# Three of eight pairs of k-tiles of the SwiGLU products as seven block products in place of eight, with casts of 2048 columns

## Chip, core and metric

The kernel runs on one core of one Trainium2 chip. The metric is device time in microseconds (us). The kernel before takes 1956.91 us, the median of three runs.

## What is computed

One layer of a streaming encoder over 256 rows of width 2048 in f32. Nearly all arithmetic is in the two SwiGLUs (inner width 5632) that open and close the layer, SwiGLU 1 and SwiGLU 2; between them lie a mixing layer (latent attention and gated linear attention) and a cross-attention to 256 memory rows.

```python
def swiglu(h, w_gate, w_up, w_down):
    return (jax.nn.silu(h @ w_gate) * (h @ w_up)) @ w_down
...
        x = x + 0.5 * swiglu(rmsnorm(x, ffn1_norm[l]), ffn1_w_gate[l], ffn1_w_up[l], ffn1_w_down[l])
...
        x = x + jnp.concatenate([o_mla, o_gla], axis=-1) @ w_out[l]
        x = x + memory_cross_attention(rmsnorm(x, mem_attn_norm[l]), rmsnorm(mem, mem_norm[l]),
...
        x = x + 0.5 * swiglu(rmsnorm(x, ffn2_norm[l]), ffn2_w_gate[l], ffn2_w_up[l], ffn2_w_down[l])
```

## The kernel before

Every large product runs in `gemm` (L114). TensorE multiplies in f32r, a rounded f32, so both factors are split into a high and a low part of that type, and three products are summed in PSUM: high by high, high by low, low by high. A k-tile is 128 rows of a weight matrix. For 256 rows of x (two blocks `b` of 128, the stationary tiles) and 1024 columns of weights (two halves `c` of 512), one k-tile costs 12 matmuls into the four PSUM banks named `acc`:

```python
L123            o, w = chunks[c]
L124            self.last_pe = nc.tensor.matmul(
```

`slab` (L92) loads two k-tiles, 1 MB, by SyncE's queue into one of three buffers `raw`, and splits each of the two:

```python
L109            self.last_act = nc.scalar.copy(out=wh, in_=src)
L110            self.last_dve = nc.vector.tensor_tensor(out=wl, in0=src, in1=wh.bitcast(F32), op=ALU.subtract)
```

ScalarE casts 1024 columns to the high part `wh`, and VectorE subtracts it from `raw` to give the low part `wl`. There are four buffers of each.

`ffn` (L369) runs a SwiGLU in two groups of inner columns, of six and five *chunks* of 512, numbered 0 to 10. A chunk multiplies all 16 k-tiles of x (its high and low parts are `hth` and `htl`) by 512 columns of gate and 512 of up: 192 matmuls. Then ScalarE evicts the gate with a Silu (L386) and VectorE multiplies by up (L388). Splitting these activations is side work, done during the next chunk: TensorE transposes them (L177), ScalarE casts (L182) and VectorE subtracts (L183), into `acth` and `actl`. After the chunks of a group *down* multiplies the group's 24 or 20 k-tiles of activations by w_down, 1024 columns of output at a time (two such gemms), and VectorE adds the result to the residual `xs` (L404). The rope tables and gains of the mixing layer are set up during chunk 2 of SwiGLU 1 (`setup_mix`): small loads issued by GpSimd, a transpose of the gains (L255), and some 30 small operations on VectorE (L328 among them).

The order on each engine's queue is fixed when the program is built: a scheduler places the instructions by its own estimate of when their inputs are there, and each engine then runs its queue in order. Buffers come from rotating pools, and a tile waits until the readers of its buffer's last content are done.

Of the kernel before, what the change touches and what calls it, by code (L numbers as in the profile page):

```python
# [50 lines left out]

class Kernel:
    def __init__(self, ctx, tc, io):
# [36 lines left out]
    def slab(self, segs, k0, nk, per):  # L90
# [13 lines left out]
        for j in range(0, nk, per):  # L104
            m = min(per, nk - j)
            wh = self.wspl.tile([P, 2 * CW], F32R, name="wh")[:, :m * width]
            wl = self.wspl.tile([P, 2 * CW], F32R, name="wl")[:, :m * width]
            src = flat[:, j * width:(j + m) * width]
            self.last_act = nc.scalar.copy(out=wh, in_=src)  # L109
            self.last_dve = nc.vector.tensor_tensor(out=wl, in0=src, in1=wh.bitcast(F32), op=ALU.subtract)  # L110
# [3 lines left out]
    def gemm(self, x, segs, chunks, ks, ahead=None, side=()):  # L114
# [15 lines left out]
        while i < n:  # L130
            if ahead:
                ahead(i)
            nk = 1 if ahead and i < 2 else min(2 * per, n - i)
            with ExitStack() as first:
                if ahead and not i:
                    for ins in self.first:
                        first.enter_context(self.tc.issue_after(ins))
                parts = self.slab(segs, ks[i], nk, per)
# [21 lines left out]
        return out  # L160

# [32 lines left out]

    def sum_sq(self, src, out, width):
# [3 lines left out]
    def new_ht(self):  # L199
        return [  # L200
            tuple(self.keep.tile([P, 4, S], F32R, name=f"ht{p}{n}") for p in "hl") for n in range(NCH)
        ]

    def norm_chunk(self, src, ht, ss, n, b, g, sq=True):

        self.split_t(src, ht[n], 0, b, 4, g + 4 * n)
        if sq:
            self.sum_sq(src, ss[:, b, n:n + 1], CW)
# [789 lines left out]
```

## Time and profile before

| | |
|---|---|
| median of three runs (lowest to highest) | 1956.91 us (1956.27 to 1957.24) |
| the profiled execution, whole | 1957.86 us |
| its span from first to last instruction | 1956.2 us |
| mean granted TensorE clock, share of full | 0.999 |
| instructions | 22341 |
| weights and other data moved | 356.05 MB, mean 182 GB/s |

The profile is of one execution: times in it are held against its own 1957.86 us, not against the median. Its views give, per engine, busy time and counts; for each group of instructions the time of one and the idle time before it with what ended it; and the chain of work that ended last, followed back from the last instruction.

### The profile page before, as it was taken

What the parts mean: (1) busy time and instruction counts of PE and PEld (TensorE: products, weight loads), DVE (VectorE), ACT (ScalarE), POOL (GpSimd) and SP (SyncE); (2) the same over time, 40 slices, a digit from 0 to 9 for tenths busy, and PEclk for the clock granted to TensorE, in tenths of its full rate; (3) what the DMA queues carried; (4) which work ended last, traced back from release to release, by engine and by line L of the source; (5) the groups of instructions that cost most, each with busy time, mean ns of one, the idle gap of its engine ahead of it and who ended that gap; (6) DMA issues with size and microseconds to landing.
All of it is one profiled execution on the core that took longest, in us unless ns stands there. A gap on an engine that the chain in (4) does not pass through costs nothing.

```text
span 1956.2 us, 22341 instructions
## 1 busy us (share of the span) xinstructions
PE 1940.9 (99%) x8712; PEld 1584.2 (81%) x8712; DVE 1015.8 (52%) x1272; ACT 906.8 (46%) x1277; POOL 58.5 (3%) x114
## 2 busy tenths in 40 slices
PE   8999999999999999999999999999999999999999
PEld 6888888888888888788778878888888888888887
DVE  5555544444545455555565656554444445454443
ACT  6444443334444445665556665544444334444432
POOL 2000000000000000120100020000000000000000
PEclk9999999999999999999999999999999999999999
DMA  7555655555555545554336544555555555565563
GB/s 263 188 186 186 193 194 177 189 194 186 190 186 191 193 173 176 178 159 153 129 128 208 177 153 155 193 180 188 192 193 184 183 192 194 186 192 183 193 208 115
DMA packets 148075, 356.05 MB, mean 182 GB/s; under 512 B 11018, under 2 KB 11120, under 8 KB 147968
## 3 DMA queue, kind: packets, MB, share of 16 engines
q1 hardware_dynamic: 147360, 354.07, 54.8%
q8 instruction: 68, 1.11, 0.2%
q0 software_dynamic: 608, 0.55, 0.1%
q14 instruction: 39, 0.32, 0.0%
HBM read 352.48 MB, written 2.10 MB: 181 GB/s over the span
## 4 chain that ended last, share of the span: by engine, by line
PE 98%; DMA 1%; ACT 1%; POOL 0%; DVE 0%; issue 0%; SPq 0%; ACTq 0%
PE acc L124 93%; PE bank L177 2%; PE bank L743 0%; PE bank L598 0%; PE bank L579 0%; PE bank L742 0%; DMA raw<-in_ffn_w_up_dram 0%; PE bank L797 0%; ACT junk L197 0%; PE bank L806 0%; DMA m<-in_mem_dram 0%; ACT wh L109 0%; PE bank L673 0%; PE bank L808 0%; PE bank L883 0%
## 5 line engine op out<-in xcount | busy, mean ns | idle before, releaser
L110 DVE TENSOR_TENSOR wl<-raw,wh 128x1024 fp32r<-128x1024 f32 (+2 forms) x668 | 809.5, 1216 | 789.0 <-ACT wh L109 787.8
L109 ACT CAST wh<-raw 128x1024 fp32r<-128x1024 f32 (+2 forms) x668 | 695.0, 1046 | 906.6 <-PE acc L124 865.7
L124 PE MATMUL acc<-wh,hth 128*128 128x512 f32 (+1 forms) x1696 | 667.5, 394 | 2.5 <-ACT wh L109 2.5
L124 PE MATMUL acc<-wl,hth 128*128 128x512 f32 (+1 forms) x1696 | 659.1, 389 | 0.0
L124 PE MATMUL acc<-wh,htl 128*128 128x512 f32 (+1 forms) x1696 | 540.6, 388 | 0.0
L124 PEld LDWEIGHTS acc<-wh,hth 128*128 128x128 f32 x1696 | 319.3, 188 | 72.6 <-issue 3.7
L124 PEld LDWEIGHTS acc<-wh,htl 128*128 128x128 f32 x1696 | 318.3, 188 | 65.2
L124 PEld LDWEIGHTS acc<-wl,hth 128*128 128x128 f32 x1696 | 319.4, 188 | 63.0
L124 PE MATMUL acc<-wh,acth 128*128 128x512 f32 x704 | 280.2, 398 | 0.0
L124 PE MATMUL acc<-wl,acth 128*128 128x512 f32 x704 | 279.0, 396 | 0.0
L124 PE MATMUL acc<-wh,actl 128*128 128x512 f32 x704 | 227.1, 396 | 0.0
L124 PEld LDWEIGHTS acc<-wh,actl 128*128 128x128 f32 x704 | 132.7, 188 | 32.3
L124 PEld LDWEIGHTS acc<-wh,acth 128*128 128x128 f32 x704 | 132.6, 188 | 31.9
L124 PEld LDWEIGHTS acc<-wl,acth 128*128 128x128 f32 x704 | 132.6, 188 | 31.7
L388 DVE SCALAR_TENSOR_TENSOR t<-acc,sm,t 128x512 f32<-128x512 f32 x44 | 33.0, 750 | 51.8 <-PE acc L124 46.4
L188 ACT ACTIVATE hth<-bank,gains 128x128 fp32r<-128x128 f32 x128 | 42.3, 366 | 25.8 <-DVE htl L191 19.8
L386 ACT ACTIVATE t<-acc,sm 128x512 f32<-128x512 f32 x44 | 30.4, 691 | 49.7 <-PE acc L124 49.7
L191 DVE SCALAR_TENSOR_TENSOR htl<-bank,gains,hth 128x128 fp32r<-128x128 f32 x128 | 40.2, 345 | 13.2 <-ACT hth L188 13.0
L404 DVE SCALAR_TENSOR_TENSOR xs<-acc,xs 128x512 f32<-128x512 f32 x32 | 21.5, 688 | 17.1 <-PE acc L124 17.1
L183 DVE TENSOR_TENSOR actl<-bank,acth 128x512 fp32r<-128x512 f32 x44 | 30.1, 683 | 0.0
L177 PEld LDWEIGHTS bank<-ident,t 128*128 128x128 f32 x188 | 23.4, 140 | 6.3
L177 PE MATMUL bank<-ident,t 128*128 128x128 f32 x188 | 28.3, 272 | 0.0
(231 smaller groups left out, 989.8 us busy)
## 6 DMA issues: line engine op xcount, KB each, us to landing
raw<-in_ffn_w_down_dram SPq DMA_DIRECT2D x88, 1024.0 KB, 5.1
raw<-in_ffn_w_gate_dram SPq DMA_DIRECT2D x175, 512.0 KB, 3.8
raw<-in_ffn_w_up_dram SPq DMA_DIRECT2D x175, 512.0 KB, 4.7
raw<-in_w_in_dram SPq DMA_DIRECT2D x24, 1024.0 KB, 5.1
raw<-in_w_out_dram SPq DMA_DIRECT2D x16, 1024.0 KB, 5.2
raw<-in_w_in_dram SPq DMA_DIRECT2D x8, 832.0 KB, 4.6
raw<-in_mem_w_k_dram SPq DMA_DIRECT2D x4, 1024.0 KB, 5.1
raw<-in_mem_w_q_dram SPq DMA_DIRECT2D x4, 1024.0 KB, 5.1
```

Of the source, the lines that this page charges most:

```text
L109: self.last_act = nc.scalar.copy(out=wh, in_=src)
L110: self.last_dve = nc.vector.tensor_tensor(out=wl, in0=src, in1=wh.bitcast(F32), op=ALU.subtract)
L124: self.last_pe = nc.tensor.matmul(out=out[b][c][:, :w], lhsT=high, rhs=part[:, o:o + w], start=start, stop=stop)
L177: nc.tensor.transpose(out=t[:, j * P:(j + 1) * P], in_=src[:, j * P:(j + 1) * P], identity=self.ident)
L183: nc.vector.tensor_tensor(out=tl[:, j0:j0 + nj, bs], in0=tv, in1=hv.bitcast(F32), op=ALU.subtract)
L188: h = nc.scalar.activation(out=hv, in_=tv, func=AF.Copy, scale=gv)
L191: nc.vector.scalar_tensor_tensor(out=tl[:, j0 + j, bs], in0=tv, scalar=gv, in1=hv.bitcast(F32), op0=ALU.mult, op1=ALU.subtract)
L386: nc.scalar.activation(out=sg, in_=out[b][0], func=AF.Silu, scale=r)
L388: nc.vector.scalar_tensor_tensor(out=a, in0=out[b][1], scalar=r, in1=sg, op0=ALU.mult, op1=ALU.mult)
L404: nc.vector.scalar_tensor_tensor(out=xc, in0=out[b][c], scalar=0.5, in1=xc, op0=ALU.mult, op1=ALU.add)
```

## The change

Two neighbouring k-tiles form a *pair*. A pair of weight tiles, with two k-tiles as rows and two halves of 512 as columns, and a pair of tiles of x, with two blocks of rows and two k-tiles as columns, are 2 x 2 block matrices. The kernel before multiplies them as eight block products, which with three products of parts each are 24 matmuls. The change takes three of a chunk's eight pairs (1, 3 and 5; in the last group's down two of six: 1 and 3) in seven block products, p1 to p7 (Strassen's scheme in Winograd's form), 21 matmuls. These pairs are called *mixed*, the others *plain*.

- A mixed pair needs sums of weight blocks: VectorE makes four of them, in f32, in one buffer `wsum` (L204 two at once, L209, L210, each from the one before). ScalarE casts 1536 columns of the raw blocks and 2048 columns of the sums, and VectorE makes their low parts (L125). The low part of the sums is called *sum-low* below.
- It needs sums of blocks of x and of the activations too. `split_pair` (L338) makes them from transposed blocks in a buffer `f` on VectorE (L370 to L373) and casts and subtracts seven blocks of 128 columns at once (L375). There is one buffer `f`.
- Three products (p2, p3, p4) go straight to an `acc` bank; p1, p5, p6 and p7 are summed over the mixed pairs in four more banks. After the last mixed pair `middle` (L292) copies p1 (L298, ScalarE) and forms four combinations (L297, VectorE), which are added when the `acc` banks are evicted (L575, L578).
- Eviction of a chunk becomes: VectorE subtracts from the gate banks (L575), ScalarE takes the Silu, VectorE adds to the up banks (L578) and multiplies both (L580).
- All casts take 2048 columns, one plain pair, where they took 1024. Plain and mixed pairs take turns by a list: 1, 0, 3, 2, 5, 4, 6, 7. The first chunk of SwiGLU 1, whose x and weights are still arriving, takes 0, 2, 4, 6, 1, 3, 5, 7.
- SwiGLU's inner columns run in three groups of four, four and three chunks, so there are six down gemms for four.
- The weight buffers `wh` and `wl` (four each, now of 2048 columns) belong to a pool of each stage and no longer to the whole kernel; the mixing layer has its own, and its own buffers `work`.
- `setup_mix` moves from chunk 2 of SwiGLU 1 to chunk 10, the last one, where its operands lie in a buffer of the activations and its rows of gains in `f`.

```diff
+MIXED8, ORDER8 = (1, 3, 5), (1, 0, 3, 2, 5, 4, 6, 7)
+MIXED6, ORDER6 = (1, 3), (1, 0, 3, 2, 4, 5)
+ORDER_FIRST = (0, 2, 4, 6, 1, 3, 5, 7)
...
         self.wraw = pool("wraw", 3)
-        self.wspl = pool("wspl", 4)
-        self.tmp = pool("tmp", 3)
+        self.tmp = pool("tmp", 1)
...
+    def parts(self, src, width):
+        nc, n = self.nc, src.shape[-1]
+        wh = self.wspl.tile([P, width], F32R, name="wh")[:, :n]
+        wl = self.wspl.tile([P, width], F32R, name="wl")[:, :n]
+        self.last_act = nc.scalar.copy(out=wh, in_=src)
+        self.last_dve = nc.vector.tensor_tensor(out=wl, in0=src, in1=wh.bitcast(F32), op=ALU.subtract)
+        return wh, wl
...
+    MIXED = [("p1", 2, "B11"), ("p5", 4, "t1"), ("p7", 0, "t3"), ("p6", 5, "t2"),
+             ("p4", 1, "t4"), ("p2", 3, "B21"), ("p3", 6, "B22")]
+    PLACE = {"p3": (0, 0), "p2": (0, 1), "p4": (1, 1)}
...
+    def mixed_parts(self, raw):
+        nc = self.nc
+        q = [raw[:, i * CW:(i + 1) * CW] for i in range(4)]
+        t = self.wsum.tile([P, 4 * CW], F32, name="wsum")
+        t1, t3, t2, t4 = (t[:, i * CW:(i + 1) * CW] for i in range(4))
+        nc.vector.tensor_tensor(
+            out=t[:, :2 * CW].rearrange("p (j n) -> p j n", j=2),
+            in0=raw[:, CW:3 * CW].rearrange("p (j n) -> p j n", j=2),
+            in1=q[0].unsqueeze(1).broadcast_to([P, 2, CW]), op=ALU.add,
+        )
+        nc.vector.tensor_tensor(out=t2, in0=t1, in1=q[2], op=ALU.add)
+        nc.vector.tensor_tensor(out=t4, in0=t2, in1=q[3], op=ALU.add)
+        forms = {}
+        for src, names in ((raw[:, CW:], ("B11", "B22", "B21")), (t, ("t1", "t3", "t2", "t4"))):
+            wh, wl = self.parts(src, 4 * CW)
+            for i, name in enumerate(names):
+                forms[name] = tuple(w[:, i * CW:(i + 1) * CW] for w in (wh, wl))
+        return forms
...
+        out = [[self.acc.tile([P, CW], F32, name="acc") for _ in range(2)] for _ in range(NB)]
+        if ahead:
+            ahead(0)
+        units = []
+        for p in order:
+            units += [(p, (0,)), (p, (1,))] if ahead and not units else [(p, (0, 1))]
+        mixed = [i for i, (p, _) in enumerate(units) if xs[p][0]]
...
+        def step(u):
+            if side and not (mixed and mixed[0] <= u < mixed[-1]):
+                side.pop(0)()
...
+                raw = self.raw_pair(cols, k0 + 2 * p + kk[0], len(kk))
+                if is_mixed:
+                    forms = self.mixed_parts(raw)
+                else:
+                    wh, wl = self.parts(raw, 4 * CW)
+            if is_mixed:
+                if u == mixed[0]:
+                    extra = {name: self.bank() for name in ("p1", "p5", "p7", "p6")}
+                for name, i, form in self.MIXED:
+                    key = self.PLACE.get(name, name)
+                    bank = extra[name] if name in extra else out[key[0]][key[1]]
+                    fh, fl = forms[form]
+                    ah, al = (t[:, i * P:(i + 1) * P] for t in (xh, xl))
+                    stop = u == mixed[-1] if name in extra else last
+                    product(key, bank, ah, fh, False)
+                    product(key, bank, ah, fl, False)
+                    product(key, bank, al, fh, stop)
+                if u == mixed[-1]:
+                    middle(extra)
+                    step(u)
+                continue
...
+    def middle(self, extra):
+        nc = self.nc
+        p1, u3 = (self.sums.tile([P, CW], F32, name="su", bufs=4) for _ in range(2))
+        u4, v = (self.sums.tile([P, CW], F32, name="sg", bufs=2) for _ in range(2))
+        add = lambda out, a, b: nc.vector.tensor_tensor(out=out, in0=a, in1=b, op=ALU.add)
+        nc.scalar.copy(out=p1, in_=extra["p1"])
+        add(u4, extra["p6"], p1)
+        add(u3, extra["p7"], u4)
+        add(v, extra["p5"], u3)
+        add(u4, extra["p5"], u4)
+        return p1, u4, u3, v
...
+        f = self.tmp.tile([P, 7 * P], F32, name="f")
...
+        a21, a22, a11, a12, s5, s6, s3 = (f[:, i * P:(i + 1) * P] for i in range(7))
+        nc.vector.tensor_tensor(out=s5, in0=a22, in1=a21, op=ALU.subtract)
+        nc.vector.scalar_tensor_tensor(out=s6, in0=s5, scalar=-1.0, in1=a11, op0=ALU.mult, op1=ALU.subtract)
+        nc.vector.tensor_tensor(out=s3, in0=s6, in1=a12, op=ALU.add)
+        nc.vector.tensor_tensor(out=a21, in0=a11, in1=a21, op=ALU.subtract)
+        nc.scalar.copy(out=th, in_=f)
+        nc.vector.tensor_tensor(out=tl, in0=f, in1=th.bitcast(F32), op=ALU.subtract)
...
-        rows = self.tmp.tile([G_ROWS, P], F32, name="rows", bufs=1)
+        rows = self.tmp.tile([P, 7 * P], F32, name="f")[:G_ROWS, :P]
...
+            self.wsum, self.wspl, self.sums, acts_pool = pool("wsum", 1), pool("wspl", 4), pool("sums", 1), pool("acts", 1)
+            for c0, c1 in ((0, 4), (4, 8), (8, 11)):
+                pairs = 2 * (c1 - c0)
+                mixed, order = (MIXED8, ORDER8) if pairs == 8 else (MIXED6, ORDER6)
                 acts = []
                 for c in range(c0, c1):
-                    o = c * CW
-                    if c == 2:
+                    if c == 10:
                         marks = self.last_act.ins, self.last_dve.ins
-                    out = self.gemm(
-                        x, [(wg, o, CW), (wu, o, CW)], [(0, CW), (CW, CW)], list(range(KD)), None if c else ahead
+                    mid = []
...
+                    out = self.pair_gemm(
+                        ht, [(wg, c * CW), (wu, c * CW)], 0, ORDER8 if c else ORDER_FIRST,
+                        lambda extra: mid.extend(self.middle(extra)), None if c else ahead,
                     )
-                    act = tuple(pool.tile([P, 4, S], F32R, name=f"act{p}") for p in "hl")
+                    p1, u4, u3, v = mid
+                    sg, a = (u4, v), (p1, u3)
...
+                        tt(out=sg[b], in0=out[b][0], in1=sg[b], op=ALU.subtract)
+                        nc.scalar.activation(out=sg[b], in_=sg[b], func=AF.Silu, scale=rstd()[:, b:b + 1])
+                    for b in range(NB):
+                        tt(out=a[b], in0=out[b][1], in1=a[b], op=ALU.add)
+                    for b in range(NB):
+                        stt(out=a[b], in0=a[b], scalar=rstd()[:, b:b + 1], in1=sg[b], op0=ALU.mult, op1=ALU.mult)
+                    for p in (0, 1):
+                        m = 2 * (c - c0) + p in mixed
...
+                if side and c1 == 11:
...
+                        side(acts_pool.tile([P, 7 * P], F32R, name="actmh", bufs=3).bitcast(F32))
...
+                    def middle(extra):
+                        p1, u4, u3, v = self.middle(extra)
+                        for b, c, s, f in ((0, 1, p1, 0.5), (0, 0, u4, -0.5), (1, 1, u3, 0.5), (1, 0, v, -0.5)):
+                            stt(out=xc[b][c], in0=s, scalar=f, in1=xc[b][c], op0=ALU.mult, op1=ALU.add)
+                    out = self.pair_gemm(acts, [(wd, n * CW), (wd, (n + 1) * CW)], 4 * c0, order, middle)
+                    for c in range(2):
+                        for b in range(NB):
+                            stt(out=xc[b][c], in0=out[b][c], scalar=0.5, in1=xc[b][c], op0=ALU.mult, op1=ALU.add)
...
+        def ahead(u):
+            if u < NCH:
                 with ExitStack() as after:
-                    if n:
-                        self.load_x(n)
+                    if u:
+                        self.load_x(u)
```

Where the instructions stand before and now, by each engine's queue:

VectorE, before, at the border of two gate/up chunks: L388 evicts the chunk that ends, L110 makes low parts of 1024 columns, L183 those of the activations.

```order
L388 SCALAR_TENSOR_TENSOR t<-acc,sm_488,t 128x512 x2
L110 TENSOR_TENSOR wl<-raw,wh 128x1024 x4
L183 TENSOR_TENSOR actl<-bank,acth 128x4x128
L110 TENSOR_TENSOR wl<-raw,wh 128x1024
L183 TENSOR_TENSOR actl<-bank,acth 128x4x128
L110 TENSOR_TENSOR wl<-raw,wh 128x1024 x11
```

VectorE, now, in a gate/up chunk of SwiGLU 1, first listing: two mixed pairs and the plain pair behind each. L204, L209 and L210 make the sums of the weights, and L125 makes low parts.

```order
L204 TENSOR_TENSOR wsum<-raw 128x1024
L125 TENSOR_TENSOR wl<-raw,wh 128x1536
L209 TENSOR_TENSOR wsum<-wsum,raw 128x512
L210 TENSOR_TENSOR wsum<-wsum,raw 128x512
L125 TENSOR_TENSOR wl<-wsum,wh 128x2048
L125 TENSOR_TENSOR wl<-raw,wh 128x2048
L204 TENSOR_TENSOR wsum<-raw 128x1024
L125 TENSOR_TENSOR wl<-raw,wh 128x1536
L209 TENSOR_TENSOR wsum<-wsum,raw 128x512
L210 TENSOR_TENSOR wsum<-wsum,raw 128x512
L125 TENSOR_TENSOR wl<-wsum,wh 128x2048
L125 TENSOR_TENSOR wl<-raw,wh 128x2048
```

For each mixed pair three additions and two low parts stand where two low parts stood before, and the low part that reads `wsum` comes right behind the last sum.

TensorE, now, in a gate/up chunk, second listing: pair 3 (`hth3`, `htl3`) and the beginning of pair 2 (`hth2`). `wh_1245` and `wl_1246` are the parts of pair 3's raw blocks, `wh_1249` and `wl_1250` those of its sums, `wh_1277` the high part of pair 2.

```order
L236 MATMUL acc_1163<-wh_1245,hth3_122 128x512
L236 MATMUL acc_1163<-wl_1246,hth3_122 128x512
L236 MATMUL bank_1183<-wh_1249,hth3_122 128x512
L236 MATMUL bank_1184<-wh_1249,hth3_122 128x512
L236 MATMUL bank_1185<-wh_1249,hth3_122 128x512
L236 MATMUL acc_1166<-wh_1249,hth3_122 128x512
L236 MATMUL acc_1163<-wh_1245,htl3_123 128x512
L236 MATMUL acc_1163<-wh_1277,hth2_120 128x512
L236 MATMUL acc_1164<-wh_1277,hth2_120 128x512
L236 MATMUL acc_1165<-wh_1277,hth2_120 128x512
L236 MATMUL bank_1183<-wl_1250,hth3_122 128x512
L236 MATMUL bank_1183<-wh_1249,htl3_123 128x512
```

Before, a k-tile's products stood together in the order of the code (high by high, high by low, low by high). Now the products with the high part of the sums stand first, then three of pair 2, and only then those with the sums' low part.

VectorE, now, at the border of the first chunk of SwiGLU 1 and the second, third listing: L297 forms the combinations of the first chunk, L575 to L580 evict it, L209, L210 and L125 belong to the second chunk's weights.

```order
L209 TENSOR_TENSOR wsum<-wsum,raw 128x512
L297 TENSOR_TENSOR sg<-bank,su 128x512
L297 TENSOR_TENSOR sg<-bank,sg 128x512
L575 TENSOR_TENSOR sg<-acc,sg 128x512 x2
L578 TENSOR_TENSOR su<-acc,su 128x512 x2
L580 SCALAR_TENSOR_TENSOR su<-su,sm_342,sg 128x512 x2
L210 TENSOR_TENSOR wsum<-wsum,raw 128x512
L125 TENSOR_TENSOR wl<-raw,wh 128x1536
L125 TENSOR_TENSOR wl<-wsum,wh 128x2048
L125 TENSOR_TENSOR wl<-raw,wh 128x2048
```

The evictions and gate products of the first chunk stand ahead of the low parts of the second chunk's first pairs; before, L388 stood ahead of them as well, twice and alone.

## Rows read from the trace of the kernel before

**Rows 1.** The page: busy time (share, count) by engine, chain that ended last.
```profile
PE 1940.9 (99%) x8712; PEld 1584.2 (81%) x8712; DVE 1015.8 (52%) x1272; ACT 906.8 (46%) x1277; POOL 58.5 (3%) x114
...
PE 98%; DMA 1%; ACT 1%; POOL 0%; DVE 0%; issue 0%; SPq 0%; ACTq 0%
```

**Rows 2.** Waits: engine, tile, line, releaser: us in all, times, longest.
```profile
ACT wh L109 <- PE acc L124: 865.7, 523, 3.9
DVE wl L110 <- ACT wh L109: 787.8, 551, 5.0
```

**Rows 3.** The chain in time: start us, us, what, count of instructions.
```profile
63.55 0.44 PE bank L177 x4
...
111.67 40.82 PE acc L124 x180
...
156.15 40.82 PE acc L124 x180
...
289.88 175.50 PE acc L124 x756
...
1023.96 36.54 PE acc L124 x156
```

**Rows 4.** Windows, gate/up, down: us; PE, PEld, DVE, ACT, POOL busy; clock; DMA.
```profile
200.00:241.00 41.00, 41.00 (x184) 34.02 (x183) 20.23 (x18) 17.57 (x18) 0.00 (x0) 1.00 0.58 183
290.00:424.00 134.00, 134.00 (x575) 107.90 (x574) 64.02 (x57) 50.27 (x49) 0.00 (x0) 1.00 0.54 188
```

**Rows 5.** Groups by form: count, then busy us, mean ns, idle before.
```profile
L110 DVE TENSOR_TENSOR wl<-raw,wh 128x1024 fp32r<-128x1024 f32 x644 | 785.4, 1224 | 763.5 <-ACT wh L109 762.3
L110 DVE TENSOR_TENSOR wl<-raw,wh 128x768 fp32r<-128x768 f32 x8 | 7.6, 956 | 11.4 <-ACT wh L109 11.4
L109 ACT CAST wh<-raw 128x1024 fp32r<-128x1024 f32 x644 | 674.1, 1052 | 884.9 <-PE acc L124 848.8 <-DVE xs L404 19.3 <-issue 8.5
L109 ACT CAST wh<-raw 128x768 fp32r<-128x768 f32 x8 | 6.6, 832 | 8.0 <-PE acc L124 5.9 <-issue 2.1
L627 DVE TENSOR_TENSOR t<-t,g_out 128x512 f32<-128x512 f32 x4 | 2.7, 684 | 0.8 <-ACT t L618 0.8
L404 DVE SCALAR_TENSOR_TENSOR xs<-acc,xs 128x512 f32<-128x512 f32 x32 | 21.5, 688 | 17.1 <-PE acc L124 17.1
L388 DVE SCALAR_TENSOR_TENSOR t<-acc,sm,t 128x512 f32<-128x512 f32 x44 | 33.0, 750 | 51.8 <-PE acc L124 46.4 <-ACT wh L109 2.3 <-PE bank L255 2.0
L182 ACT CAST acth<-bank 128x512 fp32r<-128x512 f32 x44 | 25.6, 581 | 0.0
L328 DVE SCALAR_TENSOR_TENSOR ang<-whole,ang 128x128 f32<-128x128 f32 x8 | 2.3, 290 | 0.2
```

**Rows 6.** Timeline of VectorE and ScalarE: start us, us, instruction, count, idle before.
```profile
147.84 2.35 DVE L110 TENSOR_TENSOR wl<-raw,wh 128x1024 fp32r<-128x1024 f32 x2
...
97.78 0.62 DVE L328 SCALAR_TENSOR_TENSOR ang<-whole,ang 128x128 f32<-128x128 f32 x2
...
301.17 1.05 ACT L109 CAST wh<-raw 128x1024 fp32r<-128x1024 f32 x1 [1.76 <-PE acc L124]
...
302.25 1.23 DVE L110 TENSOR_TENSOR wl<-raw,wh 128x1024 fp32r<-128x1024 f32 x1 [1.59 <-ACT wh L109]
```

**Rows 7.** Timeline of ScalarE over the first 30 us.
```profile
8.78 1.04 ACT L109 CAST wh<-raw 128x1024 fp32r<-128x1024 f32 x1 [1.85 <-DMA raw<-in_ffn_w_up_dram]
...
14.32 1.05 ACT L109 CAST wh<-raw 128x1024 fp32r<-128x1024 f32 x1 [2.58 <-DMA raw<-in_ffn_w_up_dram]
...
18.76 1.05 ACT L109 CAST wh<-raw 128x1024 fp32r<-128x1024 f32 x1 [0.69 <-DMA raw<-in_ffn_w_up_dram]
```

**Rows 8.** GpSimd's loads in groups, and a weight load on the page.
```profile
L246 POOL DMA_DIRECT2D rows<-in_mla_k_norm_dram x1 | 0.5, 492 | 2.1 <-DMA g_out<-in_gla_out_norm_dram 2.1
L246 POOL DMA_DIRECT2D rows<-in_mem_q_norm_dram x1 | 0.5, 487 | 1.5 <-DMA rows<-in_mix_norm_dram 1.5
...
raw<-in_ffn_w_down_dram SPq DMA_DIRECT2D x88, 1024.0 KB, 5.1
```

More of the change, by code (lines that the diff above doesn't have):

```diff
@@ L105, in slab, with gemm @@
             m = min(per, nk - j)
[L106 to L110, printed above, removed]
+            wh, wl = self.parts(flat[:, j * width:(j + m) * width], 2 * CW)
             parts += [(wh[:, i * width:(i + 1) * width], wl[:, i * width:(i + 1) * width]) for i in range(m)]
         return parts
-    def gemm(self, x, segs, chunks, ks, ahead=None, side=()):
+    def parts(self, src, width):
[5 more added lines that the diff above has]
+        return wh, wl
+    def gemm(self, x, segs, chunks, ks, side=()):
         nc = self.nc
@@ L130, in gemm @@
         while i < n:
[L131 to L138, printed above, removed]
+            nk = min(2 * per, n - i)
+            parts = self.slab(segs, ks[i], nk, per)
             last = i + nk == n
@@ L197, in sum_sq, with new_ht, norm_pair @@
         self.nc.scalar.activation(out=junk[:, :width], in_=src, func=AF.Square, accum_out=out)
[L199 to L208, printed above, removed]
+    def new_ht(self, mixed=()):
+        pairs = []
+        for p in range(KD // 2):
+            width = (7 if p in MIXED8 else 4) * P
+            tiles = [self.keep.tile([P, width], F32R, name=f"ht{h}{p}") for h in "hl"]
+            pairs.append((p in mixed, *(t if p in mixed else t[:, :4 * P] for t in tiles)))
+        return pairs
+    def norm_pair(self, src, ht, p, g):
+        at = lambda b, k: src(b)[:, (p % 2 * 2 + k) * P:(p % 2 * 2 + k + 1) * P]
+        self.split_pair(at, ht[p], g + 2 * p)
     def rstd(self, ss):
@@ L312, in setup_mix_body @@
         parts.append(rest)
-        ang, whole, trig = (pool.tile([P, 2, NB, HALF], F32, name=name) for name in ("ang", "whole", "trig"))
-        turns = pool.tile([P, 2, NB, HALF], I32, name="turns")
+        ang, whole, trig, turns = (
+            room[:, 164 + i * 128:164 + (i + 1) * 128].rearrange("p (i b f) -> p i b f", i=2, b=NB) for i in range(4)
+        )
+        turns = turns.bitcast(I32)
         flat = lambda t: t.rearrange("p i b f -> p (i b f)")
@@ L426, in mix_and_cross @@
         wide = lambda c0, *side: self.gemm(x, [(w_in, c0, 2 * CW)], halves, range(KD), side=side)
-        with ExitStack() as outs:
+        with ExitStack() as weights, ExitStack() as outs:
+            pool = lambda name, bufs: weights.enter_context(self.tc.tile_pool(name=name, bufs=bufs, reuse_waits="tile"))
+            self.wspl, self.work = pool("wspl", 4), pool("work", 3)
             pool = outs.enter_context(right("omt"))
@@ L686, in steps @@
                 for c in range(2):
[L687 removed]
+                    rope = self.work.tile([P, 2, ROPE], F32, name="rope")
                     self.rotate(qs[b][c][:, :, NOPE:], rope, 0, b, 2)
@@ L720, in steps @@
                 for c in range(2):
-                    rope = self.tmp.tile([P, 2, ROPE], F32, name="rope")
+                    rope = self.work.tile([P, 2, ROPE], F32, name="rope")
                     for hh in range(2):
```

192 lines of the change are left out of this document (128 added, 64 removed).

## Prediction

> **What bounds the kernel now.** I read the page first: TensorE is busy 99% of the span and makes up 98% of the chain that ended last [rows 1]. Busy time alone proves little, because matmuls overlap, so the view of waits came next: ScalarE's casts wait for TensorE to give weight buffers back (865.7 us), and VectorE's low parts wait for those casts (787.8 us) [rows 2]. Both converters are ahead and throttled by TensorE. The chain in time gives TensorE's price: 180 gate/up matmuls in 40.82 us, 0.2268 us each, and one chunk of gate and up (192 matmuls and eight transposes) starts every 44.48 us (156.15 less 111.67) [rows 3]. The 756 matmuls from 289.88 are 576 of down and 180 of gate/up, so down costs (175.50 - 40.82)/576 = 0.2338 each [rows 3]. The granted clock is 1.00 of 2.4 GHz in both [rows 4]; I don't know why the two differ. VectorE is busy 20.23 of 41 us in a gate/up stretch and 64.02 of 134 in down [rows 4]. That half-empty VectorE is what the change draws on.
>
> **What the change removes.** A pair of k-tiles costs 24 matmuls, a mixed pair 21. Each SwiGLU has 11 chunks x 3 mixed pairs and 2 x (3 + 3 + 2) in down; both together 66 + 32 = 98 mixed pairs, 294 matmuls: 198 x 0.2268 + 96 x 0.2338 = 67.3 us, if nothing waits.
>
> **What it adds on VectorE.** The trace has no operation of 2048 or 1536 columns. The rows of 768 and 1024 columns lie 1.047 ns a column apart, so the low part takes 2.30 us at 2048 and 1.76 at 1536; two of 1024 bound the first above at 2.45, and the column rate without a fixed part below at 2.14. ScalarE's casts give 0.859 ns a column, 1.93 us at 2048 [rows 5]. The weight sums are additions of f32 in SBUF; a multiplication of that form takes 0.684 us at 512 columns, and the low part at 1024 gives 1.22 [rows 5]. VectorE instructions overlap by 0.09 us (two of 1.22 in 2.35), unless the second needs the first: two dependent ones of 0.29 fill 0.62 [rows 5, 6].
>
> A plain pair then occupies VectorE 2.21 us. A mixed pair takes 1.13 (double sum), 1.67 (low part of the raw tiles), 0.72 and 0.69 (the dependent sums) and 2.21 (low part of the sums): 6.4 us, more than TensorE's 21 x 0.2268 = 4.76. Moreover, the first order listing shows nothing between the last sum and the low part of the sums for two of the three mixed pairs. VectorE has to stand still there while ScalarE casts the sums: 1.93 us and 0.03 to 0.04 at each handover (a cast from 301.17 for 1.05 us, the low part at 302.25) [rows 6], 2.0 together.
>
> One gate/up chunk of VectorE: 3 x 6.4 + 5 x 2.21 + 2 x 2.0 for weights, four combinations after the last mixed pair (2.5), four evictions at 0.60 and two products with the gate at 0.66 (0.69 and 0.75 less 0.09; 3.7), and splitting a plain and a mixed activation pair (2.7): 43 us. TensorE needs 183 x 0.2268 + 0.87 = 42.4. So **VectorE becomes about as long as TensorE**, and I have to walk through a chunk. Zero is the end of TensorE's previous chunk.
>
> VectorE evicts the last bank until 0.8, makes pair 1's sum-low until 3.1, finishes the gate product and has pair 0's low part at 6.0. TensorE meets the sum-low after 14 products (3.2) and pair 0's low after 12 more (5.9): a wait of 0.1. Then 20 products, to 10.5. VectorE's four steps for pair 3 end at 10.1 and the cast at 12.05; ScalarE then casts pair 2 until 14.0. The second order listing shows three products of pair 2 *ahead* of pair 3's sum-low, so TensorE stops at 13.2 for 0.8. It finishes pair 2 at 21.3. Pair 5: steps until 20.7, cast until 22.7, copy of p1 (0.58, as the cast out of PSUM in [rows 5]) and cast of pair 4 until 25.15; TensorE, 13 products and four transposes on, is there at 24.7 and waits 0.45. The rest (79 products and four transposes) runs free: 43.75. VectorE's remaining work from 24.9 is 18.3 us and ends with TensorE. The period is 43.75, not 42.4: **0.73 us less than before**. Eight chunks of a SwiGLU are like this; chunks 4 and 8 have no splitting, and I give them 42.7 (-1.8). 20 chunks: 2 x (8 x 0.73 + 2 x 1.8) = **-18.9**.
>
> Down has no gate product: VectorE needs 41 us for eight pairs, TensorE 183 x 0.2338 = 42.8, and the same walk leaves about 0.4 of waits. Before, that part took 192 x 0.2338 = 44.9, so -1.7, and -1.2 in the first of each group, which has splitting: 8 x 1.45 = 11.6. The four of six pairs gain 1.4 - 0.4 = 1.0 each: **-15.6** in all.
>
> **What it costs elsewhere.** The first chunk's order is 0, 2, 4, 6, then the three mixed pairs in a row, at 8.2 us of VectorE each including the unhidden casts. In SwiGLU 1 the transfers delay the plain pairs as well: before, casts that waited for them began at 8.78, 14.32 and 18.76, behind 1.5, 3 and 4 MB [rows 7]. Pair 1's raw data is now the seventh MB, at that pace near 31 us, so the last sum-low comes at about 57 and the chunk ends at 63.7. Before, it ended at 63.55 less 24 matmuls, 58.1 [rows 3]: +5.6. The third listing shows what follows: the evictions and gate products come ahead of the next chunk's low parts, so TensorE's first matmuls wait 4.4. **+10.0**. In SwiGLU 2 the weights are prefetched: 4.4 + 1.1 less the 2.0 saved, **+3.5**.
>
> The setup of rope tables moves from chunk 2, where VectorE had idle time, to the border of chunk 10 and down. Its loads reuse the one buffer `f`, free only 5.7 us before chunk 10 ends; ten GpSimd loads at 0.5 us and two waits near 2 us [rows 8] land 5 us after it, where TensorE's transpose of the gains has stood for 3.5. Some 7 us of small VectorE operations then lie among the weights of a VectorE-paced gemm; I count 4. **+7.5**. The weight buffers, once one pool for the whole kernel, now change hands at the two stage borders: **+4** (0 to 10).
>
> At nothing: DMA, the same bytes; a 1024 KB load lands in 5.1 us [rows 8], and each of the three raw buffers is free at least 6.9 us before the walk needs its next content. ScalarE, under 30 of 43 us. The renamed pools of the middle part.
>
> The sum: -18.9 - 15.6 + 10.0 + 3.5 + 7.5 + 4 = -9.5. The profiled execution took 1957.86 (1956.2 of span and 1.7 around it), 0.95 over the median of the runs. 1957.9 - 9.5 - 0.95 = 1947.4; I say **1948**.
>
> **A rule that speaks against the change.** The pair in [rows 6] starts 1.13 us apart, less than one duration. The Trainium skill (VectorE: DVE Perf Modes, "The DRAIN you can't avoid") says that a following operation starts only when the pipe has emptied. By that, 35 operations a chunk would cost 3 us more. For operations that don't depend on each other the trace disagrees; few in it follow so closely with other engines' waits between them.
>
> **Rivals.**
> *TensorE stays the bound (0.14).* If the waits I found are covered, because the low parts run nearer 2.14 or TensorE's reordered products cover more, all 67.3 go, less 5 for the first chunks and 7.5 for setup and borders: 1902. Against it: the two casts per chunk that VectorE must wait out.
> *Matmuls of gate/up at the other pitch (0.20), slower.* All weight buffers and activations lie at new addresses. In the trace 0.2268 holds for one kind of stationary tile only (`ht`); activations and `omt` have 0.2338 and 36.54/156 = 0.2342 [rows 3]. If gate/up falls to that, 183 x 0.007 = 1.28 us a chunk, of which 0.6 to 1.28 shows; 22 chunks give +13 to +28, 1970 in the middle. It decides from 0.003 us a matmul.
> *Every VectorE operation occupies its full duration (0.06).* Chunks near 46.9, down 45.3 for eight pairs: about +45 in these, with the costs above 2028.
> *VectorE paces and the sum holds (0.52)*: 1948, itself 1935 to 1962 (half a microsecond on each of 34 gemms is 17). The remaining 0.08: a start or border much worse than I count, around 1965.
>
> **How the numbers follow.** A measurement of this kernel tells 0.2% (4 us) from nothing. Of the likeliest case about 0.35 lies under 1953, 0.12 within 4 us of 1957 and 0.05 above; TensorE as the bound is faster; the other cases are slower but for 0.02 each of faster and same. Faster 0.51, same 0.14, slower 0.35. The range leaves out the last of the full-duration case and half of the TensorE case: 1908 to 1984.
>
> **What would show it.** Right: gate/up chunks 43 to 44.5 us apart; VectorE busy over 85% there; its low parts of `wsum` each after 2 us of idleness released by ScalarE's cast; TensorE idle 1 to 2 us a chunk, ended by casts and low parts, and 4 us at the start of chunk 1 and of the third down group. Wrong: chunks of 42.4 and no TensorE idleness; a pitch other than 0.227 in gate/up; dependent VectorE operations that take longer than their rows; long waits for DMA or for a PSUM bank.

## The result, and the profile after

The changed kernel takes 1969.63 us (median of four runs, 1968.53 to 1970.24) against 1957.08 for the kernel before on the same chip: a ratio of 1.0064, 95% interval 1.0046 to 1.0081. It is slower by 12.5 us, where 1948 and a gain were forecast. The profiled execution has a span of 1968.5 us. Of all executions below one, of the kernel with the pad and the spread order, took 6233 us; it is left out, and the median of that run is of the other four.

The page of the changed kernel, busy time by engine and the chain that ended last; it answers to [rows 1]:

```profile
span 1968.5 us, 21848 instructions
...
PE 1915.9 (97%) x8418; PEld 1528.0 (78%) x8418; DVE 1555.6 (79%) x1691; ACT 1006.4 (51%) x1088; POOL 59.6 (3%) x114
...
PE 68%; DVE 15%; ACT 7%; issue 6%; DMA 3%; POOL 1%; SPq 0%; ACTq 0%; DVEq 0%
```

294 matmuls are gone, TensorE's busy time fell by 25 us only, and the chain is no longer TensorE's alone: VectorE, ScalarE and the time in which the engine on the chain waited for nothing that the profile shows (issue) hold 28% of it. Its waits, where [rows 2] had both converters throttled by TensorE:

```profile
ACT wh L124 <- DVE wsum L210: 412.8, 73, 10.1
DVE wl L125 <- ACT wh L124: 275.6, 172, 3.9
```

Now ScalarE waits for VectorE's last sum of the weights, and VectorE for ScalarE's cast of it: each stands while the other works. The groups by form on VectorE and ScalarE, which answer to [rows 5]:

```profile
L125 DVE TENSOR_TENSOR wl<-raw,wh 128x2048 fp32r<-128x2048 f32 x165 | 376.9, 2285 | 8.4 <-ACT wh L124 8.0
L125 DVE TENSOR_TENSOR wl<-wsum,wh 128x2048 fp32r<-128x2048 f32 x98 | 224.5, 2290 | 140.4 <-ACT wh L124 140.4
L125 DVE TENSOR_TENSOR wl<-raw,wh 128x1536 fp32r<-128x1536 f32 x98 | 171.6, 1751 | 0.0
...
L204 DVE TENSOR_TENSOR wsum<-raw 128x1024 f32<-128x1024 f32 x98 | 119.3, 1217 | 0.0
L210 DVE TENSOR_TENSOR wsum<-wsum,raw 128x512 f32<-128x512 f32 x98 | 67.5, 689 | 2.4
...
L124 ACT CAST wh<-wsum 128x2048 fp32r<-128x2048 f32 x98 | 187.1, 1909 | 491.3 <-DVE wsum L210 412.8 <-PE acc L236 78.5
```

The durations are those that were worked out (2.29 for 2.30, 1.75 for 1.76, 1.22 for 1.22, 0.69, 1.91 for 1.93). The second row is the point: 140.4 us of idleness ahead of 98 low parts of the sums, all of it ended by ScalarE's cast. On VectorE's timeline, pairs 5 and 4 of a gate/up chunk of SwiGLU 2:

```profile
1384.99 1.22 DVE L204 TENSOR_TENSOR wsum<-raw 128x1024 f32<-128x1024 f32 x1
1386.12 1.75 DVE L125 TENSOR_TENSOR wl<-raw,wh 128x1536 fp32r<-128x1536 f32 x1
1387.79 0.68 DVE L209 TENSOR_TENSOR wsum<-wsum,raw 128x512 f32<-128x512 f32 x1
1388.51 0.69 DVE L210 TENSOR_TENSOR wsum<-wsum,raw 128x512 f32<-128x512 f32 x1
1391.25 2.29 DVE L125 TENSOR_TENSOR wl<-wsum,wh 128x2048 fp32r<-128x2048 f32 x1 [2.05 <-ACT wh L124]
1393.54 2.29 DVE L125 TENSOR_TENSOR wl<-raw,wh 128x2048 fp32r<-128x2048 f32 x1
```

From one L204 to the next (1374.32, pair 3, to 1384.99, pair 5) a mixed and a plain pair take 10.67 us. TensorE's price, as pieces of the chain in time of the changed kernel; it answers to [rows 3]:

```profile
105.12 14.00 PE acc L236 x60
...
193.09 11.22 PE acc L236 x48
```

60 gate/up matmuls take 14.00 us, 0.2333 each, where they took 0.2268. In down some stretches have 0.2268 now (from 487.0 to 494.0 us of the trace they start 0.227 apart), where it was 0.2338. The two pitches have changed places. In gate/up the long pitch hides most of the stall: TensorE is busy 89.78 of the 90 us from 1320 to 1410, its own 183 x 0.2333 + 0.87 make 43.6, and chunks take 43.4 to 44.4.

The stages, from the starts of their first matmuls in the two traces (us):

| stretch | before | changed | difference | forecast |
|---|---|---|---|---|
| SwiGLU 1, chunks 0 and 1 | 92.5 | 108.4 | +15.9 | +9.3 |
| SwiGLU 2, chunks 0 and 1 | 90.0 | 98.1 | +8.1 | +2.8 |
| the other 18 chunks | 798.7 | 790.0 | -8.7 | -17.4 |
| all of down, with setup and stage borders | 500.3 | 495.7 | -4.6 | -4.1 |
| start, middle part, end | 474.7 | 476.3 | +1.6 | 0 |
| sum | | | +12.3 | -9.5 |

The sum of the differences is that of the spans (1968.5 - 1956.2). The forecasts are the terms of the prediction, put together by these stretches. Chunk 10 of SwiGLU 1 is counted as long as that of SwiGLU 2; the 3.2 us up to down's first matmul behind it go to the fourth line. Of the 21.8 us between forecast and result 11.9 lie in the first chunks and 8.7 in the other 18. In the changed kernel chunk 2 starts at 118.96 and 1324.81, with twelve matmuls into the banks of p1, p5, p7 and p6. The expectations below count chunks from the first matmul into `acc`, 2.8 us later, and therefore have 18.7 and about 11 for the first two lines.

### The profile page after: what moved, and what is told of

Same layout as the page of the kernel before. It is cut to its first block, busy times and chain, and to the rows that moved or that the text cites. A ratio compares the mean times of both kernels' runs of the same rounds, so it can differ in the third digit from the quotient of the medians.

```text
span 1968.5 us, 21848 instructions
## 1 busy us (share of the span) xinstructions
PE 1915.9 (97%) x8418; PEld 1528.0 (78%) x8418; DVE 1555.6 (79%) x1691; ACT 1006.4 (51%) x1088; POOL 59.6 (3%) x114
## 4 chain that ended last, share of the span: by engine, by line
PE 68%; DVE 15%; ACT 7%; issue 6%; DMA 3%; POOL 1%; SPq 0%; ACTq 0%; DVEq 0%
PE acc L236 38%; PE acc L138 18%; DVE wl L125 8%; PE bank L236 7%; ACT wh L124 6%; DMA raw<-in_ffn_w_up_dram 2%; DVE wsum L204 2%; PE bank L345 2%; DVE wsum L210 1%; DVE wsum L209 1%; DVE su L580 1%; DVE su L578 1%; PE bank L943 0%; PE bank L798 0%; PE bank L779 0%
## 5 line engine op out<-in xcount | busy, mean ns | idle before, releaser
L125 DVE TENSOR_TENSOR wl<-raw,wh 128x2048 fp32r<-128x2048 f32 (+4 forms) x405 | 716.5, 1771 | 136.9 <-ACT wh L124 135.3
L124 ACT CAST wh<-raw 128x2048 fp32r<-128x2048 f32 (+4 forms) x405 | 593.0, 1489 | 230.5 <-PE acc L138 128.4
L124 ACT CAST wh<-wsum 128x2048 fp32r<-128x2048 f32 x98 | 187.1, 1909 | 491.3 <-DVE wsum L210 412.8
L236 PE MATMUL acc<-wh,hth 128*128 128x512 f32 x1078 | 416.6, 402 | 7.3 <-ACT wh L124 7.0
L236 PE MATMUL acc<-wl,hth 128*128 128x512 f32 x1078 | 416.6, 398 | 0.6 <-DVE wl L125 0.6
L236 PE MATMUL acc<-wh,htl 128*128 128x512 f32 x1078 | 370.2, 397 | 0.0
L125 DVE TENSOR_TENSOR wl<-wsum,wh 128x2048 fp32r<-128x2048 f32 x98 | 224.5, 2290 | 140.4 <-ACT wh L124 140.4
L236 PE MATMUL acc<-wl,actph 128*128 128x512 f32 x448 | 168.1, 396 | 3.1 <-DVE wl L125 3.1
L204 DVE TENSOR_TENSOR wsum<-raw 128x1024 f32<-128x1024 f32 x98 | 119.3, 1217 | 0.0
L138 PE MATMUL acc<-wh,hth 128*128 128x512 f32 (+1 forms) x288 | 114.1, 398 | 0.0
L138 PE MATMUL acc<-wl,hth 128*128 128x512 f32 (+1 forms) x288 | 111.0, 387 | 0.0
L236 PEld LDWEIGHTS acc<-wh,actph 128*128 128x128 f32 x448 | 83.9, 188 | 26.6 <-ACT wh L124 9.8
```

The source lines that it names most:

```text
L138: self.last_pe = nc.tensor.matmul(out=out[b][c][:, :w], lhsT=high, rhs=part[:, o:o + w], start=start, stop=stop)
L204: nc.vector.tensor_tensor(out=t[:, :2 * CW].rearrange("p (j n) -> p j n", j=2), in0=raw[:, CW:3 * CW].rearrange("p (j n) -> p j n", j=2), ...
L236: self.last_pe = nc.tensor.matmul(out=bank, lhsT=high, rhs=part, start=key not in seen, stop=stop)
```

## Experiments

Two theories stood at the start. **A**: matmuls got a longer pitch from the tiles' addresses, and at each mixed pair VectorE stands while ScalarE casts the sums; both stretch gate/up and above all the first chunks. **B**: VectorE is short of time as a whole, so that neither the pitch nor a single stall matters. The other rival was that late transfers make the first chunks long. All times are medians; beside the three sets of runs the kernel before had 1956.9, 1956.7 and 1956.5.

**The pitch.** In the built program the weight tiles of the changed kernel lie 192 B past the tiles of x modulo 256 (108864 and 26240), and at the same place modulo 256 as the activations (186688). In the kernel before, it is the other way round: x (38528) lies as the weights (95872) do, the activations (152544) lie 96 off. One pad moves the weights, sums and activations against x:

```diff
-        self.small.tile([P, 8], F32, name="pad_left")
+        self.small.tile([P, 24], F32, name="pad_left")
```

> The changed kernel with one pad longer by 64 B, so that weight tiles, sums and activations lie 64 B further on and the tiles of x stay: weights and x are then congruent modulo 256 B, as weights and activations already are. Theory A (the pitch of matmuls depends on how the addresses of the stationary and the moving tile lie to each other, and gate/up is bound by TensorE at the longer pitch): gate/up goes from 0.2335 to 0.2268 us a matmul, chunks of 44.4 become 43.1 to 43.8, and the mixing layer's four gemms with x gain 5; 1969.6 becomes 1937 to 1952. Theory B (VectorE paces the chunks, the pitch is hidden in its waits): the pitch falls but chunks stay near 44.2; 1961 to 1966. If the pitch does not depend on addresses: no change, 1968 to 1971.

Measured: 1955.26, 14.4 less than the changed kernel; 0.9991 of before, interval 0.9981 to 1.0. That is just above the upper end of what theory A gave. Chunks of 43.6 fall to 42.5, but those of 44.4 to 44.0 only: there the stall shows where the pitch no longer hides it.

The same edit in the kernel before, where the activations move by 160 B and the tiles at the right end (`omt`, `ogt`) by 96:

```diff
+        self.small.tile([P, 40], F32, name="pad_left")
+        pad = ctx.enter_context(tc.tile_pool(name="pad", bufs=1, side="right"))
+        pad.tile([P, 24], F32, name="pad_right")
```

> The kernel before with its activations 160 B further on and the mixing layer's right-hand tiles 96 B lower, nothing else: activations then lie congruent to the weights modulo 512 B, as x does. Theory A (addresses set the pitch): down goes from 0.2342 to 0.2268 us a matmul, 2112 of them, 15 us less, and some 5 in the mixing layer; 1935 to 1944. Rival (the pitch belongs to activations, to down's single transfer of 1024 KB, or to the evictions): no change, 1956 to 1958.

Measured: 1939.06, a ratio of 0.9904 (0.9889 to 0.9919). Nothing but addresses has changed, and the kernel is 18 us faster.

And the pad 192 B longer (`[P, 56]`), which puts weights and x 128 B apart:

> The changed kernel with the pad 192 B longer instead of 64: weights and x then lie 128 B apart modulo 256, where they lay 192 apart (changed kernel, long pitch) and 0 (first run, short pitch). If congruence modulo 128 is what counts, gate/up has 0.2268 and the run takes 1953 to 1958 like the first; if modulo 256 or more, 0.233 and 1966 to 1972 like the changed kernel.

Measured: 1964.2, a little under the range of the second case. A piece of the chain in time of each of the three, with the pad of 64 B, in the kernel before with its pads (576 of down and 180 of gate/up, as in [rows 3]), and with 192 B:

```profile
103.37 13.62 PE acc L236 x60
```
```profile
291.03 171.43 PE acc L127 x756
```
```profile
102.90 14.00 PE acc L236 x60
```

13.62/60 = 0.2270; (171.43 - 40.82)/576 = 0.2268 for down, which was 0.2338 with the same instructions; 14.00/60 = 0.2333. Distances of 0 and 256 B modulo 512 have the short pitch; 96, 128 and 192 B modulo 256 have the long one. So in these runs the short pitch goes with a stationary and a moving tile that are congruent modulo 256 B; modulo 128 isn't enough. Other distances were not tried.

**The first chunk's order.**

```diff
-ORDER_FIRST = (0, 2, 4, 6, 1, 3, 5, 7)
+ORDER_FIRST = (0, 2, 1, 4, 3, 6, 5, 7)
```

> The changed kernel with the first chunk's order 0, 2, 1, 4, 3, 6, 5, 7: a plain pair between each two mixed ones, in place of three mixed pairs in a row. Theory A (the row of mixed pairs is what costs 18.7 us in SwiGLU 1 and about 11 in SwiGLU 2: four weight buffers hold two mixed pairs, casts wait for TensorE, VectorE waits for casts, and TensorE's clock falls in the idle time): 16 to 24 us less, 1946 to 1954. Theory B (late transfers and the setting up of x make the first chunk long): SwiGLU 2 gains its 8 to 10, SwiGLU 1 less than 3; 1957 to 1962. If both are due to something else: 1966 to 1970.

Measured: 1963.4, 6.2 less. None of the three cases. Chunks 0 and 1 fell by 5.8 in SwiGLU 1 and 3.3 in SwiGLU 2, so the row of three mixed pairs is 9.1 of the 24.0 us that they had grown by (the middle part took 1.5 longer in this run). The theory B of this expectation, late transfers, is out by its sizes, since it had SwiGLU 1 gain less than 3. The run with all three edits below moves the same bytes and takes 89.2 for chunks 0 and 1 of SwiGLU 2, where the kernel before takes 90.0, so late transfers are not most of what made SwiGLU 2's first chunk long. In the spread order the stall was still there: at 1248.52 and 1259.20 of this trace the low parts of the sums begin after 2.03 and 2.05 us of idleness. I had put the price on the row and not on the stall in each pair of it.

**No mixed pairs.** All pairs plain; what is left is the casts of 2048 columns, the three groups, the addresses and the place of the setup. These lines turn the mixed pairs off; the rest of the edit drops the sums and the combinations and keeps the widths of all tiles:

```diff
-MIXED8, ORDER8 = (1, 3, 5), (1, 0, 3, 2, 5, 4, 6, 7)
-MIXED6, ORDER6 = (1, 3), (1, 0, 3, 2, 4, 5)
+MIXED8, ORDER8 = (), (1, 0, 3, 2, 5, 4, 6, 7)
+MIXED6, ORDER6 = (), (1, 0, 3, 2, 4, 5)
...
```

> The changed kernel with no mixed pair: all eight block products everywhere, no weight sums, no combinations; casts of 2048 columns, three groups, pools, addresses and the place of the setup stay as in the changed kernel. Theory A (gate/up bound by TensorE at the longer pitch): chunks of 192 x 0.2335 + 0.87 = 45.7, down at 0.2275, no stall in the first chunks; 1957.1 + 27 - 13 + 8 = 1979, 1972 to 1986, so the block products by themselves gain about 10 over this. Theory B (the casts of 2048 and the groups cost nothing, the sums are what costs): near 1957 or below, 1945 to 1962.

Measured: 1971.75 (theory A's end, a little below its range). The block products as they stand gain 2.1 of the 67 us that their matmuls are worth. Two gemms of down over eight pairs take 88.0 us plain and 88.4 mixed (88.67 in the expectations, by their count): nothing is gained there. Four chunks of gate/up take 181.8 plain and 175.7 mixed.

**The stall.** One edit on VectorE's queue: both low parts of a mixed pair are held back behind the last sum. The low part of the raw blocks then lies in the time of ScalarE's cast; the work is the same.

```diff
-        nc.vector.tensor_tensor(out=t4, in0=t2, in1=q[3], op=ALU.add)
+        last_sum = nc.vector.tensor_tensor(out=t4, in0=t2, in1=q[3], op=ALU.add).ins
...
-            wh, wl = self.parts(src, 4 * CW)
+            with self.tc.issue_after(last_sum):
+                wh, wl = self.parts(src, 4 * CW)
```

> The changed kernel with one edit on VectorE's queue: for a mixed pair the low part of the raw blocks is held back until after the last sum, so that it lies in the time in which ScalarE casts the sums (a stall of 2.05 us in the trace of the changed kernel). Theory A (that stall, at every mixed pair where nothing stands between, paces mixed pairs at 10.67 us for a mixed and a plain one against TensorE's 10.2 to 10.5): the stall falls to about 0.3, a mixed and a plain pair take VectorE 9.0, TensorE becomes the bound; down 88.7 a pair of gemms to 85 to 86, gate/up 175.4 a group to 174.4 to 175, the first chunks 5 to 8 less each; 1930 to 1950. Theory B (VectorE is short of time as a whole, the stall only moves to another place): 1960 to 1969.

Measured: 1920.75, 48.9 less than the changed kernel, a ratio to before of 0.9816 (0.9802 to 0.9831). More than theory A's range; B is out. VectorE's timeline and the page's chain of this run:

```profile
1345.61 1.22 DVE L204 TENSOR_TENSOR wsum<-raw 128x1024 f32<-128x1024 f32 x1
1346.87 0.69 DVE L209 TENSOR_TENSOR wsum<-wsum,raw 128x512 f32<-128x512 f32 x1
1347.59 0.69 DVE L210 TENSOR_TENSOR wsum<-wsum,raw 128x512 f32<-128x512 f32 x1
1348.20 1.75 DVE L125 TENSOR_TENSOR wl<-raw,wh 128x1536 fp32r<-128x1536 f32 x1
1351.20 2.29 DVE L125 TENSOR_TENSOR wl<-wsum,wh 128x2048 fp32r<-128x2048 f32 x1 [1.24 <-ACT wh L124]
```
```profile
PE 95%; DVE 2%; ACT 1%; DMA 1%; POOL 0%; issue 0%; SPq 0%; ACTq 0%; DVEq 0%
```

TensorE has the chain again, and VectorE is so far ahead that it waits for weight buffers (1.24 us here, behind a cast that waited itself). Two gemms of down take 84.0, four chunks 173.4.

**All three edits, and what each is worth beside the others.**

> All three edits so far together: the pad of 64 B more, the first chunk's plain pairs between the mixed ones, the low part of the raw blocks behind the last sum. Theory A (with the stall gone TensorE is the bound and each matmul that is saved counts): gate/up chunks 42.4 to 42.8, down pairs 85 to 86; 1905 to 1925. Theory B (VectorE paces): the gains of the first two runs alone, 1944 to 1950.

Measured: 1887.48, a ratio of 0.9643 (0.9627 to 0.9659): 17.5 us below the lower end of the expectation, and 3.6% faster than the kernel before. Chunks take 42.43 us, which is 183 x 0.2268 and 0.87 for transposes (42.4) and next to nothing else. The page and a mixed and a plain pair on VectorE:

```profile
PE 1862.6 (99%) x8418; PEld 1526.8 (81%) x8418; DVE 1556.6 (83%) x1691; ACT 1016.7 (54%) x1088; POOL 62.4 (3%) x114
...
PE 93%; ACT 3%; DVE 2%; issue 1%; DMA 1%; POOL 1%; SPq 0%; ACTq 0%; DVEq 0%
```
```profile
1272.77 1.22 DVE L204 TENSOR_TENSOR wsum<-raw 128x1024 f32<-128x1024 f32 x1
...
1277.50 2.29 DVE L125 TENSOR_TENSOR wl<-wsum,wh 128x2048 fp32r<-128x2048 f32 x1 [0.39 <-ACT wh L124]
1279.71 2.28 DVE L125 TENSOR_TENSOR wl<-raw,wh 128x2048 fp32r<-128x2048 f32 x1
1281.91 1.22 DVE L204 TENSOR_TENSOR wsum<-raw 128x1024 f32<-128x1024 f32 x1
```

9.14 us from L204 to L204 in place of 10.67, while TensorE needs 45 x 0.2268 = 10.2. VectorE's busy time is the same as in the changed kernel (1556.6 and 1555.6): it never was short of time.

> The pad of 64 B and the first chunk's spread order, without the edit of VectorE's queue: what the stall for the cast of the sums costs when matmuls have the short pitch. If the three edits add up: 1955.3 less 6.2, 1949; the run with all three took 1887.5, so the stall would cost 61 here against 49 at the long pitch, because TensorE gets to the sums sooner. If spread order and pad gain on the same wait: 1953 to 1956.

Measured: 1949.0. The pad and the order add up, and the stall is worth 61.5 us at the short pitch (1949.0 - 1887.5) against 49 at the long one.

> The pad of 64 B and the low part of the raw blocks behind the last sum, with the first chunk's three mixed pairs in a row again. Without the stall such a row costs VectorE 6.6 us a mixed pair against TensorE's 4.8. If the row still costs in both SwiGLUs: 4 to 8 more than the run with all three edits, 1891 to 1896; if the stall was all that made the row slow: 1886 to 1890.

Measured: 1894.22, so the row of mixed pairs in the first chunks costs 6.7 by itself.

> The run with all three edits, but activations are never mixed: down takes eight block products for all its pairs, and activations are split plainly; gate/up keeps its three mixed pairs. Theory A (TensorE is the bound everywhere): slower than the run with mixed down by 96 matmuls of 0.2275, 22 us, less 2 for the plain splitting; 1925 to 1945. Theory B (VectorE paces down, where the products of the changed kernel gained nothing against plain: 88.67 to 88.04 a pair of gemms): as fast or faster than it, by 0 to 8.

Measured: 1907.23, 19.8 more than with mixed down; theory A's difference of 20, from a lower base than its range supposed. The products of down gain nothing with the stall and, without it, 19.8 of the 96 x 0.2268 = 21.8 us that they save.

> The changed kernel with no mixed pair and the pad of 64 B more: eight block products everywhere, casts of 2048 columns, three groups, all large matmuls at the shorter pitch. What the block products are set against when the pitch is out of the way. By the pitch alone: 1971.8 less 22 x 192 x 0.0063 and 5 in the mixing layer, 1936 to 1943; if the slow chunks of the plain run had another cause, above 1960.

Measured: 1943.34, as the pitch alone gives. Set against this, the block products of the run with all three edits gain 55.9 of the 294 x 0.2268 = 66.7 us that they save. Against the kernel before with its pads (1939.06) the run with all three edits gains 51.6.

## Why the prediction failed

**Right.** What the change saves on TensorE, the durations of the new operations, and the stall: 65 of the 98 low parts of the sums begin after some 2 us of idleness that ScalarE's cast ends, two of three as forecast. The rival that VectorE's operations occupy their full duration is out: an operation that doesn't need the last one's result starts 0.09 before its end here too (1.22 us from 1384.99, then 1386.12). The Trainium skill (VectorE: DVE Perf Modes, "The DRAIN you can't avoid") says that the next operation does not start until the pipe has emptied, and in the same paragraph that one that is not held starts earlier. The prediction gave the first half alone; this trace agrees with the second for such operations. For a sum that needs the one before, 0.04 us lie between (0.68 from 1387.79, then 1388.51), as forecast. VectorE is busy for 37.3 to 39.0 us of a chunk of 43.4 to 44.4, as the 43 less its stalls had it.

Two steps failed, each a fixed term of the sum. By what undoing it is worth the second is the larger: 14.4 us with the pad, beside 9.4 that the first chunks take over the forecast even then.

**The first: the price of the first chunks** (+10.0 and +3.5 forecast; with chunk 1 counted in, +15.9 and +8.1 measured in place of +9.3 and +2.8). These two make 11.9 of the 21.8 us between forecast and result. The forecast had the order of events: the last sum-low was put at 57; it began at 56.29 and was done at 58.58. From there on it counted TensorE at its full clock and at the short pitch. Windows of the changed kernel's first 100 us (us; PE, PEld, DVE, ACT and POOL busy; granted clock; DMA):

```profile
10.00:40.00 30.00, 29.48 (x127) 23.71 (x128) 23.63 (x35) 25.11 (x42) 1.19 (x2) 1.00 0.77 271
40.00:55.00 15.00, 11.43 (x46) 8.03 (x44) 11.82 (x10) 4.72 (x5) 0.00 (x0) 1.00 0.30 105
55.00:65.00 10.00, 8.08 (x22) 6.07 (x23) 7.13 (x6) 4.43 (x3) 0.00 (x0) 0.66 0.63 204
65.00:70.00 5.00, 3.85 (x17) 2.78 (x15) 4.71 (x9) 1.34 (x2) 0.00 (x0) 1.00 0.05 16
70.00:80.00 10.00, 6.84 (x19) 5.00 (x20) 9.63 (x8) 5.07 (x3) 0.00 (x0) 0.66 0.41 122
80.00:100.00 20.00, 20.00 (x87) 16.10 (x87) 15.07 (x12) 11.29 (x7) 0.00 (x0) 1.00 0.61 201
```

TensorE idles 3.6 us between 40 and 55, and the granted clock then stands at 0.66 on average from 55 to 65 and again from 70 to 80: two levels, 2.4 and 1.2 GHz, and the lower one for some 6.8 of each 10 us. In that time a matmul takes nearly twice as long: the chain has six from 59.77 in 2.56 us, 0.43 each. The chunk's last matmul into `acc` ended at 68.64 instead of 63.7. The wait behind it was the forecast's, 4.15 us for 4.4, but the matmuls after it ran at the lower clock again:

```profile
68.46 0.39 PE L236 MATMUL bank<-wh,hth 128*128 128x512 f32 x1
73.00 0.79 PE L236 MATMUL bank<-wl,hth 128*128 128x512 f32 x1 [4.15 <-DVE wl L125]
73.59 0.63 PE L236 MATMUL bank<-wh,htl 128*128 128x512 f32 x1
```

The clock of the kernel before is 1.00 in all these windows, and so it is from 10 to 100 us in the run with all three edits, where chunks 0 and 1 of SwiGLU 1 take 95.6 and those of SwiGLU 2 89.2. The lower clock thus came with the waits and went with them. How much of the 11.9 is the clock's I can only estimate, since no run had the waits without the clock: fourteen matmuls from 58.12 to 64.26 and five from 75.66 to 77.95 would have taken 4.0 us less at 0.2333, and fifteen in SwiGLU 2 (1265.48 to 1269.15, 1279.90 to 1282.99) 3.3 less. That is 7.3 at most. The pitch is 2.5 of it: the pad alone took 2.3 and 0.2 off these chunks, the edit of the stall alone 7.7 and 4.1, the spread order alone 5.8 and 3.3.

**The second: the pitch of gate/up.** The sum had chunks at 43.75 by a walk that used 0.2268 us a matmul, and the long pitch stood as a rival with 0.20. The rival is what happened: 0.2333, so that the other 18 chunks gained 8.7 and not 17.4. A pitch other than 0.227 in gate/up was on the prediction's own list of signs of being wrong. Its price is measured by the pad: 14.4 us, at the lower end of the +13 to +28 that I gave it, and 11.0 of it lie in these 18 chunks (790.0 to 779.0, where the forecast had 781.3). With the pad, four chunks take 173.3; the walk had given 3 x 43.75 + 42.7 = 174.0 for them. So the walk was sound for the pitch that it assumed. What it missed is that the pitch can be read off the addresses: a rule that both traces and the runs with pads now bear out. A slip in the same term is smaller: it set every chunk against 44.48, but the kernel before too has one without splitting in each SwiGLU (chunk 6, 43.5), so 1.9 of the -18.9 were never there.

**Down and setup came out by luck** (-4.6 measured, -4.1 forecast). -15.6 was forecast from the products and +11.5 for setup and borders. Down gained only 5.3 us in SwiGLU 2 (244.0 us for 249.3), and the run with no mixed pair gained more (242.5): the gain goes with the activations' new addresses, and the products' was eaten by the stall. In the walk I had left about 0.4 us of waits per gemm of eight pairs; with the fix, two such gemms take 83.9 instead of 88.4, so it was 2.2 in each. On the other side, SwiGLU 1's last chunk and its down take 118.2 us and SwiGLU 2's 111.6, so setup and borders cost about 6.6 in place of 11.5.

**What was in hand and not used.** The stall of 2.0 us was in the prediction as a fact of the queue order, at two of three mixed pairs. I put it into VectorE's total of 43 us, found that about equal to TensorE's 42.4, and walked on; an order that fills it was one line away, and it is worth 49 to 61.5 us. The rival "TensorE stays the bound" (1902) is what the kernel becomes once it is filled and the pitch is short again (1887.48, and 1894.22 with the first order).

## What to carry to other kernels

When an operation hands its result to another engine and takes it back, look at what stands between on its own queue: a dependent pair with nothing in between stalled for the other engine's whole duration here (2.05 us idle for a cast of 1.91), and a total of busy time (79% here) doesn't show it; the idle time ahead of one form of instruction does. Before a change of buffers is costed by durations, compare the addresses of the stationary and moving tiles modulo 256 B before and after: 3% of a matmul's time hung on it here, in both directions, and one pad set it right. A saving on the bounding engine is worth what is left after the new waits; run it first against the same kernel without the saving (1971.75 here), not only against the old one.

## What the runs showed of the hardware

The pitch of back-to-back f32r matmuls of 512 columns is 0.2268 us where the stationary and the moving tile start at the same place modulo 256 B, and 0.232 to 0.234 where they lie 96, 128 or 192 B apart modulo it, for x and for activations, in the kernel before, the changed one and the experiments on pads and orders. The Trainium skill (SBUF — State Buffer, "SBUF: two separate sides") says that among the engines only the port shared by GpSimd and VectorE is contended for and that TensorE never waits there. Pads alone made the kernel before 18 us faster, so if the longer pitch is a read that waits, the traces disagree; what waits, and for what, was not tried and stays open.

TensorE's clock fell to its lower level after the idle stretches of the first chunks and, for less, at the border with the setup (0.98 from 690 to 766 us); in the chunks and down gemms between, where TensorE's longest wait is 1.35 us, it is 1.00 (100 to 690 us, where VectorE is busy 513.96 of 590).
